# Modulation steps placed behind evictions, seven pairs of products ahead of the loop, and the order of transfers at the seam, in a two-block transformer kernel

## The chip, the core and the metric

One core of a Trainium2 chip runs the whole program. The metric is the device time of one execution in microseconds, lower being better. The engines are TensorE (PE, with its weight loads PEld), VectorE (DVE), ScalarE (ACT), GpSimd (POOL) and SyncE (SP, which here only issues transfers). Each has its own queue of instructions and works through it in order.

## What is computed

Two transformer blocks in float32 on 1024 tokens of width 1024. The first has three attentions, gates and an MLP; the second has an mLSTM, a pooling mixer and an MLP, and a modulation from a vector c. What matters here are the two MLPs and the modulation:

```python
    h = rmsnorm(x, g_mlp[l])
    hid = jnp.square(jax.nn.relu(jnp.einsum("bsd,df->bsf", h, w_mlp_in[l])))
    x = x + jnp.einsum("bsf,fd->bsd", hid, w_mlp_out[l])
...
    mod = c_act @ w_ada[l] + b_ada[l]          # c_act = silu(c), w_ada 1024 x 6144
    sh1, sc1, gt1, sh2, sc2, gt2 = jnp.split(mod, 6, axis=-1)
    h = _modulate(_rmsnorm(x, g_mix[l]), sh1, sc1)
```

The modulation depends on c alone and is wanted only by the second block, so the kernel works it out during the first block's MLP.

## The kernel before

A float32 product is made of three float32r products: each operand is split into a high part (a cast on ACT) and a low part (a subtraction on DVE or POOL), and hi·hi, hi·lo and lo·hi are added up in PSUM. The function `mlp` (from line 1211) holds both products of an MLP and is called twice, by block 1 with the modulation as its `tick` and by block 2 without one.

Both products are cut in 2 x 2 and done with Strassen and Winograd's seven products. In the first, each of 16 rounds m takes two blocks of 128 columns of w1 (`e1` and `e2`), and the seven products are of 12 matmuls each (128x128 by 128x512). P1 and P2 (`first_two`, line 1263) need only `e1` and the first half of the tokens, whose split is B11 and B21. The other five need sums of weights (`sums`, on POOL) and T1 to T4 and B22, which come from the second half of the tokens: T1 and B22 lie in `HT[1]`, T2 to T4 in six tiles of the tag `q`. `make_t` (line 1102) makes T1 as soon as the second half's norm is spread; its inner `rest` makes B22 and T2 to T4 and holds four of the six PSUM banks of the tag `mm` meanwhile.

So before the loop the kernel does P1 and P2 for m = 0 to 3, between them the norm's steps (`begin[0]`, `begin[1]`: column sums, then the spread of the result) and `rest`. In the loop, P1 and P2 for round m + 1 are done in round m from m = 3 on. A round with them has 84 matmuls, one without has 60. Evictions of a round are lines 1310, 1311, 1317, 1327, 1328, 1335, 1339 and 1340 (DVE), with 1274 for P2; line 1227 and 1228 are the two parts of a weight split. Each round saves seven results of 256 KB to DRAM through ACT's queue; four of them are put off until the next round (`later`).

The modulation is a generator, `ada` (line 1182). Each `next` loads one 128x512 block of w_ada through SP's queue and adds it, scaled, to a sum on DVE; after eight of them the next one turns the sum with four transposes, reduces it (line 1208) and adds the bias (line 1209). That makes 12 groups of nine steps. The MLP asks for two steps after the u2 and q12 evictions and two after q22, and for three (`tick2`) ahead of most products of the second stage. The order of each engine's queue is set by a scheduler that goes by the order in the program and by what it takes to be ready; it may take an instruction up earlier than it is written.

The second product (`for ch in range(4)`, four quarters of seven products) reads the saved results back as operands (`second`, two raw buffers of 1 MB, split at lines 1370 on ACT and 1371 on DVE and POOL in turn) and w2 in quarters (`quarter`, into the six tiles of T2 to T4). `upd` (line 1374) and `gather` add a product to x or to U and V7. x itself was saved to DRAM before the first product and comes back in 16 transfers at line 1356, ahead of the first quarter.

Of the kernel before, what the change touches and what calls it, by code (L numbers as in the profile page):

```python
# [14 lines left out]
AF = mybir.ActivationFunctionType  # L15
# [45 lines left out]
def block_kernel(ctx, tc, x, mem, positions, g_mix, w_in, b_gate, sinks, g_mem, w_mem_kv, w_proj_swa, w_proj_dsa,  # L61
# [1028 lines left out]
    def mlp_dram(pool):  # L1090
        d = {n: pool([P, NM, 512], tag=f"ml_{n}") for n in OUTS}
        d["x"] = pool([P, DC, S], tag="ml_x")
        return d
# [10 lines left out]
    def make_t(pool, dst, src, rs, gain, shift=None):  # L1104
# [22 lines left out]
        def rest():  # L1127
# [17 lines left out]
        rest_t.append(rest)  # L1145

# [6 lines left out]
    def x_cols(hf, e):  # L1153
# [8 lines left out]
        A.copy(xT[hf][:, e, :], pt)  # L1162

# [14 lines left out]

    mod = cst([P, 48], tag="mod")
    bada = cst([P, 48], tag="bada")  # L1180

    def ada(modp):
        badr = modp([48, P], tag="badr")
        nc.scalar.dma_start(badr, b_ada_2[0].rearrange("(k p) -> k p", p=P))
        pt = tp_bank()
        T.transpose(pt[:, :48], badr, ident[:48, :48])
        V.tensor_copy(bada, pt[:, :48])
        r0, _ = ROWS["c_2"]
        s_ = modp([P, 64], tag="silu")[:, :DC]
        A.activation(s_, cols[:, r0:r0 + 8], AF.Tanh, scale=0.5)  # L1190
        V.scalar_tensor_tensor(s_, s_, 1.0, cols[:, r0:r0 + 8], op0=OP.add, op1=OP.mult)
        V.tensor_scalar(s_, s_, 0.5, None, op0=OP.mult)
        for g in range(12):
            acc = modp([P, 512], tag="ada", bufs=1)
            for k in range(DC):
                w = modp([P, 512], tag="adaw", bufs=2)
                nc.sync.dma_start(w, w_ada_2[0, k * P:(k + 1) * P, halves(g)])
                if k == 0:
                    V.tensor_scalar(acc, w, s_[:, 0:1], None, op0=OP.mult)
                else:  # L1200
                    V.scalar_tensor_tensor(acc, w, s_[:, k:k + 1], acc, op0=OP.mult, op1=OP.add)
                yield
            yield
            m4 = mod[:, g * 4:(g + 1) * 4]
            pt = tp_bank()
            for j in range(4):
                T.transpose(pt[:, j * P:(j + 1) * P], acc[:, j * P:(j + 1) * P], ident)
            V.tensor_reduce(m4, pt.rearrange("p (j q) -> p j q", j=4), axis=AX.X, op=OP.add)
            V.tensor_tensor(m4, m4, bada[:, g * 4:(g + 1) * 4], op=OP.add)

    def mlp(PB, xt, d, w1, w2, scale, post, begin, middle, tick=lambda: None, gains=None, each=lambda i, e: None,
# [45 lines left out]
        def save(n, m, t_):  # L1257
            nc.scalar.dma_start(d[n][:, m, :], t_)

        def save_later():  # L1260
            while later:
                save(*later.pop(0))

        def first_two(m, e1, mid=None, eng=None):
# [5 lines left out]
            if mid:  # L1270
                mid()
# [3 lines left out]
            relu2(q11)  # L1275

# [12 lines left out]
        first_two(0, w_of(wp, 0, "wr", 2))  # L1289
        begin[0]()  # L1290
        first_two(1, w_of(wp, 2, "wr", 2), begin[1])
        first_two(2, w_of(wp, 4, "wr", 2), eng=G)
        rest_t.pop()()
        begin[2]()
        first_two(3, w_of(wp, 6, "wr", 2), eng=G)
        e1s[0] = w_of(wep, 0, "we", 2)
        sums(0)
        for m in range(NM):
# [12 lines left out]
            V.tensor_tensor(q12, p5, u2, op=OP.add)  # L1311
# [786 lines left out]
```

## Time and profile before

| | |
|---|---|
| time, median of 3 runs | 2725.16 us (2717.71 to 2726.5) |
| the profiled execution | 2721.95 us, span 2720.2 us |
| busy: PE, PEld, DVE, ACT, POOL | 93%, 77%, 69%, 44%, 36% of the span |
| mean granted clock of TensorE | 0.972 |
| moved by DMA | 338.6 MB, 124 GB/s over the span |

The first MLP runs from about 880 to 1600 us of the span, the second from about 2038 to the end at 2720. Busy time is that of one profiled execution, and its span is 1.75 us shorter than the time of the same execution. Matmuls are pipelined, so PE's busy share says when it had work and not how near it is to its peak; counts of matmuls say more. A row that names a releaser tells what ended the idle time before an instruction.

### The profile page before, as it was taken

The numbers are of one execution on the slowest core, as the hardware profiler recorded it, in microseconds if no ns is written. First come the engines' busy times: TensorE is split into PE (matmuls) and PEld (weight loads), VectorE is DVE, ScalarE is ACT, GpSimd is POOL, SyncE is SP. The second block draws the span as 40 slices with busy tenths as digits, with TensorE's granted clock in tenths as the row PEclk, the third lists the DMA queues.
The fourth block names the chain that finished last, engine by engine and source line by source line (L and its number), as shares of the span: only waits on it lengthen the run. The fifth ranks groups of instructions, "written<-read, shape, count | busy, mean of one in ns | idle before, by whom it ended". The sixth has DMA issues, their size and how long they took to land. (4 is left out here: it accounts for less than half of the span.)

```text
span 2720.2 us, 34915 instructions
## 1 busy us (share of the span) xinstructions
PE 2528.9 (93%) x12560; PEld 2107.4 (77%) x12560; DVE 1882.7 (69%) x3206; ACT 1197.9 (44%) x2218; POOL 988.1 (36%) x717
## 2 busy tenths in 40 slices
PE   7999999899999678888899979999997999989997
PEld 6899987788878566667688856888786788768886
DVE  7685878834455866676778896755658565578898
ACT  6575765335334433334433333323335554543433
POOL 3011123421002533333755661211334443476554
PEclk9999999999999889999999989999998999999999
DMA  3121022321155266666644301422343444753431
GB/s 114 53 61 40 25 79 90 89 61 41 63 183 179 78 203 200 202 204 230 220 170 155 109 24 51 156 63 70 120 152 97 160 150 159 250 204 134 170 109 62
DMA packets 275712, 338.57 MB, mean 124 GB/s; under 512 B 14268, under 2 KB 185044, under 8 KB 268372
## 3 DMA queue, kind: packets, MB, share of 16 engines
q1 hardware_dynamic: 234820, 253.65, 29.2%
q10 hardware_dynamic: 40720, 82.70, 8.3%
q8 instruction: 99, 1.62, 0.2%
q14 instruction: 73, 0.60, 0.1%
HBM read 250.25 MB, written 86.05 MB: 124 GB/s over the span
## 5 line engine op out<-in xcount | busy, mean ns | idle before, releaser
L1233 PE MATMUL mm<-h_hi,wh 128*128 128x512 f32 (+1 forms) x1136 | 455.5, 401 | 33.3 <-ACT wh L1227 17.2
L1235 PE MATMUL mm<-h_hi,wl 128*128 128x512 f32 (+1 forms) x1136 | 452.1, 398 | 10.5 <-DVE wl L1228 10.5
L1234 PE MATMUL mm<-h_lo,wh 128*128 128x512 f32 (+1 forms) x816 | 322.2, 395 | 0.0
L1233 PEld LDWEIGHTS mm<-h_hi,wh 128*128 128x128 f32 x1136 | 221.4, 195 | 82.2 <-ACT wh L1227 20.6
L1235 PEld LDWEIGHTS mm<-h_hi,wl 128*128 128x128 f32 x1136 | 220.7, 194 | 63.4 <-DVE wl L1228 18.2
L1227 ACT CAST wh<-q 128x1024 fp32r<-128x1024 f32 x116 | 121.7, 1052 | 331.7 <-PE mm L1234 297.7
L1234 PE MATMUL mm<-h_hi,wh 128*128 128x512 f32 (+1 forms) x624 | 244.8, 392 | 13.2 <-POOL h_hi L1371 13.2
L1228 DVE TENSOR_TENSOR wl<-q,wh 128x1024 fp32r<-128x1024 f32 x116 | 162.9, 1405 | 32.9 <-ACT wh L1227 31.3
L1234 PEld LDWEIGHTS mm<-h_lo,wh 128*128 128x128 f32 x816 | 158.3, 194 | 31.6
L1371 POOL TENSOR_TENSOR h_hi<-h_lo,h_hi 128x512 fp32r<-128x512 f32 x76 | 128.6, 1712 | 113.1 <-ACT h_hi L1370 107.9
L133 ACT CAST wh<-wr 128x1024 fp32r<-128x1024 f32 (+5 forms) x107 | 97.2, 911 | 149.7 <-PE mm L418 43.5
L1233 PE MATMUL mm<-q,wh 128*128 128x512 f32 x384 | 151.3, 394 | 10.4 <-DVE q L1119 10.4
L1235 PE MATMUL mm<-q,wl 128*128 128x512 f32 x384 | 150.2, 392 | 8.0 <-DVE wl L1228 8.0
L1234 PE MATMUL mm<-q,wh 128*128 128x512 f32 x384 | 150.9, 393 | 0.0
L1234 PEld LDWEIGHTS mm<-h_hi,wh 128*128 128x128 f32 x624 | 120.5, 193 | 37.9 <-POOL h_hi L1371 14.4
L1284 POOL TENSOR_TENSOR sa<-wr 128x512 f32<-128x512 f32 x32 | 41.7, 1303 | 264.8 <-DMA wr<-in_w_ff_dram 60.5
L134 POOL TENSOR_TENSOR wl<-wr,wh 128x1024 fp32r<-128x1024 f32 (+5 forms) x40 | 78.1, 1958 | 160.7 <-ACT wh L133 159.2
L1615 PE MATMUL mm<-h_hi,wh 128*128 128x512 f32 x320 | 132.0, 412 | 0.8 <-DVE kn L1648 0.8
L1617 PE MATMUL mm<-h_hi,wl 128*128 128x512 f32 x320 | 126.7, 396 | 0.0
L1371 DVE TENSOR_TENSOR h_hi<-h_lo,h_hi 128x512 fp32r<-128x512 f32 x76 | 120.4, 1605 | 8.3 <-ACT h_hi L1370 8.3
L1616 PE MATMUL mm<-h_lo,wh 128*128 128x512 f32 x320 | 125.5, 392 | 0.0
L1233 PE MATMUL mm<-h_lo,wh 128*128 128x512 f32 (+1 forms) x304 | 115.4, 380 | 0.6 <-ACT wh L1227 0.6
(589 smaller groups left out, 7006.9 us busy)
## 6 DMA issues: line engine op xcount, KB each, us to landing
h_lo<-ml_t SPq DMA_DIRECT2D x32, 1024.0 KB
adaw<-in_w_ada_dram SPq DMA_DIRECT2D x96, 256.0 KB
h_lo<-ml_q SPq DMA_DIRECT2D x24, 1024.0 KB
wr<-in_w_in_dram SPq DMA_DIRECT2D x42, 512.0 KB
wr<-in_w_out_dram SPq DMA_DIRECT2D x32, 512.0 KB
ml_t<-h_lo ACTq DMA_DIRECT2D x64, 256.0 KB
q<-in_w_mlp_out_dram SPq DMA_DIRECT2D x16, 1024.0 KB
ml_t<-x ACTq DMA_DIRECT2D x64, 256.0 KB
```

The source lines that it names most:

```text
L133: A.copy(hi, r)
L134: (eng or V).tensor_tensor(lo, r, raw(hi), op=OP.subtract)
L1227: A.copy(hi, r)
L1228: (eng or V).tensor_tensor(lo, r, raw(hi), op=OP.subtract)
L1233: mm(a, wt[0][:, k], b[0][:, k, sl], start=(k == 0), stop=False)
L1234: mm(a, wt[0][:, k], b[1][:, k, sl], start=False, stop=False)
L1235: mm(a, wt[1][:, k], b[0][:, k, sl], start=False, stop=(k == 3))
L1284: G.tensor_tensor(sa[:, 0:4], e2[:, 0:4], e2[:, 4:8], op=OP.add)
L1371: (G if c % 2 else V).tensor_tensor(lo[:, c], r[:, c], raw(hi[:, c]), op=OP.subtract)
L1615: mm(a, hi[:, k, :], r_hi, start=(k == 0), stop=False)
L1616: mm(a, hi[:, k, :], r_lo, start=False, stop=False)
L1617: mm(a, lo[:, k, :], r_hi, start=False, stop=(k == DC - 1))
```

## The change

- The modulation generator is set up earlier, and its preparation (the bias, the silu of c) is done in the steps of the projection ahead of MLP 1. It keeps two loads ahead: step i issues the load of step i + 2.
- Each step is asked for singly behind one eviction, and `tc.issue_after` ties its DVE instructions to come behind that eviction in DVE's queue. There are four per round of the first product: behind q12's two additions, q22's and u3's. In the second product they stand behind evictions in `upd`, `gather` and U's additions: 18 in the first quarter, 20 in each of the next two; what is left of the 108 steps after the loop's 64 ends in the third.
- P1 and P2 are done ahead for m = 4, 5, 6 and then 0 to 3. The results of 4 to 6 go to DRAM (`away`) and come back in rounds 3 to 5, which do no pair; from m = 6 on the loop does it as before.
- In `rest`, the subtractions for B22's and T3's low parts go from DVE to POOL (eight per MLP).
- In the last round, the six saves behind the first one are issued from POOL's queue instead of ACT's.
- x comes back in four transfers of 1 MB instead of 16 of 256 KB: its first half behind the first weights, q12 and t1, its second behind t2. In the first quarter the update of x's second half by U is therefore made later, from U.

```diff
-        def split_to(hi, lo, r):
+        def split_to(hi, lo, r, eng=V):
             A.copy(hi, r)
-            V.tensor_tensor(lo, r, raw(hi), op=OP.subtract)
+            eng.tensor_tensor(lo, r, raw(hi), op=OP.subtract)
...
             for c in range(4):
-                split_to(hi1[:, 4 + c, :], lo1[:, 4 + c, :], src(4 + c))
+                split_to(hi1[:, 4 + c, :], lo1[:, 4 + c, :], src(4 + c), G)
             for c in range(4):
-                split_to(t3[0][:, c, :], t3[1][:, c, :], src(c))
+                split_to(t3[0][:, c, :], t3[1][:, c, :], src(c), G)
...
+        def load(i):
+            if i < 12 * DC:
+                w = modp([P, 512], tag="adaw", bufs=2)
+                nc.sync.dma_start(w, w_ada_2[0, (i % DC) * P:(i % DC + 1) * P, halves(i // DC)])
+                ld.append(w)
...
+                w = ld.pop(0)
...
+                load(g * DC + k + 2)
+                yield
...
+    def tick1(after):
+        with tc.issue_after(after.ins):
+            next(ada_, None)
...
         def save(n, m, t_):
-            nc.scalar.dma_start(d[n][:, m, :], t_)
+            (nc.gpsimd if later and m == NM - 1 else nc.scalar).dma_start(d[n][:, m, :], t_)
...
+            if away:
+                nc.scalar.dma_start(d["away"][:, m - 4, 0, :], s1)
+                nc.scalar.dma_start(d["away"][:, m - 4, 1, :], q11)
...
-        first_two(0, w_of(wp, 0, "wr", 2))
+        first_of(4, away=True)
         begin[0]()
-        first_two(1, w_of(wp, 2, "wr", 2), begin[1])
-        first_two(2, w_of(wp, 4, "wr", 2), eng=G)
+        first_of(5, away=True)
+        begin[1]()
+        first_of(6, eng=G, away=True)
+        first_of(0)
         rest_t.pop()()
         begin[2]()
-        first_two(3, w_of(wp, 6, "wr", 2), eng=G)
+        first_of(1)
+        first_of(2)
+        first_of(3)
...
-                if m >= 3:
+                if m >= 6:
                     first_two(m + 1, e1s[m + 1])
+                elif m >= 3:
+                    for i, t_ in enumerate((s1s, q11s)):
+                        nc.sync.dma_start(t_[(m + 1) % 4], d["away"][:, m - 3, i, :])
...
-            V.tensor_tensor(q12, p5, u2, op=OP.add)
-            for _ in range(2):
-                tick()
+            tick(V.tensor_tensor(q12, p5, u2, op=OP.add))
...
-            V.tensor_tensor(q12, a, q12, op=OP.add)
+            tick(V.tensor_tensor(q12, a, q12, op=OP.add))
...
-            V.tensor_tensor(q22, p5, u3, op=OP.add)
+            tick(V.tensor_tensor(q22, p5, u3, op=OP.add))
...
-            for _ in range(2):
-                tick()
...
-            V.tensor_tensor(u3, a, u3, op=OP.add)
+            tick(V.tensor_tensor(u3, a, u3, op=OP.add))
...
-        for hf, es in ((1, range(4)), (0, range(8)), (1, range(4, 8))):
-            for e in es:
-                nc.sync.dma_start(xt[hf][:, e, :], d["x"][:, e, halves(hf)])
+        def x_back(hf):
+            for e0 in (0, 4):
+                nc.sync.dma_start(xt[hf][:, e0:e0 + 4, :], d["x"][:, e0:e0 + 4, halves(hf)])
...
+            if not late_ and e % 4 != 1 and (hf or e < 4):
+                tick(r)
             return t_
...
             b = second("q12", ch)
+            if not ch:
+                bt = second("t1", ch)
+                x_back(0)
             for e, wt in blocks(a11):
                 a = mm_bank()
                 product(a, wt, b)
                 gather(U[e], a, ch)
-                upd(1, e, a)
+                if ch:
+                    upd(1, e, a)
...
             b = second("t2", ch)
+            if not ch:
+                x_back(1)
             for e, wt in blocks(a11):
                 a = mm_bank()
                 product(a, wt, b)
-                V.tensor_tensor(U[e], a, U[e], op=OP.add)
+                if not ch:
+                    upd(1, e, U[e])
+                r = V.tensor_tensor(U[e], a, U[e], op=OP.add)
+                if e != 1:
+                    tick(r)
```

## Rows read from the trace of the kernel before

**Rows 1.** the page's slices of the span, 68 us each, TensorE in tenths.
```profile
PE   7999999899999678888899979999997999989997
```

**Rows 2.** busy us and count by engine and stage; PEclk, DMA share, GB/s.
```profile
884.00:986.00 102.00, 66.22 (x265) 52.09 (x264) 79.36 (x102) 39.12 (x63) 48.22 (x33) 0.82 0.38 122
986.00:1258.00 272.00, 240.05 (x995) 188.42 (x994) 194.00 (x252) 105.86 (x158) 97.84 (x69) 0.96 0.60 197
1258.00:1326.00 68.00, 52.96 (x212) 41.80 (x211) 37.58 (x44) 31.26 (x50) 36.85 (x20) 0.90 0.79 271
1326.00:1564.00 238.00, 238.00 (x1051) 197.07 (x1051) 201.94 (x200) 94.89 (x138) 146.31 (x72) 1.00 0.42 151
2040.00:2142.00 102.00, 82.78 (x343) 65.59 (x342) 73.65 (x93) 52.37 (x84) 48.52 (x34) 0.90 0.38 122
2142.00:2346.00 204.00, 204.00 (x902) 168.92 (x901) 113.50 (x139) 105.82 (x153) 92.33 (x66) 1.00 0.48 157
2346.00:2414.00 68.00, 56.44 (x229) 44.61 (x228) 43.89 (x48) 31.98 (x50) 43.59 (x22) 0.92 0.79 284
```

**Rows 3.** what TensorE waited for, 884 to 986: us in total, times, longest.
```profile
PE tp L1207 <- DVE ada L1201: 13.8, 2, 12.2
PE tp L1035 <- POOL st_r L127: 10.2, 1, 10.2
PE mm L1233 <- DVE q L1119: 5.7, 1, 5.7
```

**Rows 4.** DVE in order of time: start, us, what ran, idle before.
```profile
884.00 1.25 DVE L1191 SCALAR_TENSOR_TENSOR silu<-silu,cols 128x8 f32<-128x8 f32 x1
...
889.62 0.68 DVE L1274 TENSOR_TENSOR h_hi<-mm,h_hi 128x512 f32<-128x512 f32 x1
890.22 0.68 DVE L1025 TENSOR_REDUCE st_b<-tp 128x4 f32<-128x512 f32 x1
...
923.29 2.48 DVE L1119 TENSOR_TENSOR q<-h_lo,q 128x512 fp32r<-128x512 f32 x4
...
930.48 1.21 DVE L1228 TENSOR_TENSOR wl<-sa,wh 128x1024 fp32r<-128x1024 f32 x1
```

**Rows 5.** POOL in order of time, the same columns.
```profile
883.49 5.66 POOL L1114 TENSOR_TENSOR t<-h_hi,h_lo 128x512 f32<-128x512 f32 x4
```

**Rows 6.** what TensorE waited for, 2040 to 2142.
```profile
PE mm L1233 <- ACT x L1269: 8.2, 1, 8.2
PE mm L1233 <- DVE q L1119: 4.7, 1, 4.7
```

**Rows 7.** line 1310: count, ns min/median/max, first and last start.
```profile
L1310 DVE TENSOR_TENSOR h_hi<-mm,h_hi x3: 678/683/692, 939.2 to 980.3; 128x512 f32<-128x512 f32 x3
L1310 DVE TENSOR_TENSOR h_hi<-mm,h_hi x10: 681/684/687, 1005.1 to 1229.9; 128x512 f32<-128x512 f32 x10
L1310 DVE TENSOR_TENSOR x<-mm,x x3: 680/682/692, 2087.3 to 2120.2; 128x512 f32<-128x512 f32 x3
L1310 DVE TENSOR_TENSOR x<-mm,x x12: 685/692/693, 2138.3 to 2347.2; 128x512 f32<-128x512 f32 x12
```

**Rows 8.** DVE, 1060 to 1232: busy us, mean ns, idle before, releaser.
```profile
L1201 DVE SCALAR_TENSOR_TENSOR ada<-adaw,silu,ada 128x512 f32<-128x512 f32 x48 | 39.0, 812 | 39.5 <-DMA adaw<-in_w_ada_dram 39.0
L1209 DVE TENSOR_TENSOR mod<-mod,bada 128x4 f32<-128x4 f32 x7 | 8.7, 1249 | 0.0
```

**Rows 9.** what TensorE waited for, 1258 to 1326.
```profile
PE mm L1234 <- POOL h_hi L1371: 7.4, 1, 7.4
PE mm L1233 <- ACT wh L1227: 6.0, 1, 6.0
```

**Rows 10.** splits of operands on DVE and POOL, second product of MLP 1.
```profile
L1371 DVE TENSOR_TENSOR h_hi<-h_lo,h_hi 128x512 fp32r<-128x512 f32 x32 | 53.4, 1689 | 3.0 <-ACT h_hi L1370 3.0
L1371 POOL TENSOR_TENSOR h_hi<-h_lo,h_hi 128x512 fp32r<-128x512 f32 x32 | 55.9, 1767 | 43.4 <-ACT h_hi L1370 43.3
```

**Rows 11.** what SP's queue waited for, 1318 to 1564.
```profile
SPq L1364 <- DVE h_hi L1371: 137.4, 16, 13.2
```

More of the change, by code (lines that the diff above doesn't have):

```diff
@@ L1145, in make_t, with ada @@
         rest_t.append(rest)
+    mod = cst([P, 48], tag="mod")
+    bada = cst([P, 48], tag="bada")
+    def ada(modp):
+        badr = modp([48, P], tag="badr")
+        nc.scalar.dma_start(badr, b_ada_2[0].rearrange("(k p) -> k p", p=P))
+        yield
+        pt = tp_bank()
+        T.transpose(pt[:, :48], badr, ident[:48, :48])
+        V.tensor_copy(bada, pt[:, :48])
+        r0, _ = ROWS["c_2"]
+        s_ = modp([P, 64], tag="silu")[:, :DC]
+        A.activation(s_, cols[:, r0:r0 + 8], AF.Tanh, scale=0.5)
+        V.scalar_tensor_tensor(s_, s_, 1.0, cols[:, r0:r0 + 8], op0=OP.add, op1=OP.mult)
+        V.tensor_scalar(s_, s_, 0.5, None, op0=OP.mult)
+        yield
+        ld = []
+        def load(i):
[3 more added lines that the diff above has]
+                ld.append(w)
+        load(0)
+        load(1)
+        for g in range(12):
+            acc = modp([P, 512], tag="ada", bufs=1)
+            for k in range(DC):
+                w = ld.pop(0)
+                if k == 0:
+                    V.tensor_scalar(acc, w, s_[:, 0:1], None, op0=OP.mult)
+                else:
+                    V.scalar_tensor_tensor(acc, w, s_[:, k:k + 1], acc, op0=OP.mult, op1=OP.add)
+                load(g * DC + k + 2)
+                yield
+            yield
+            m4 = mod[:, g * 4:(g + 1) * 4]
+            pt = tp_bank()
+            for j in range(4):
+                T.transpose(pt[:, j * P:(j + 1) * P], acc[:, j * P:(j + 1) * P], ident)
+            V.tensor_reduce(m4, pt.rearrange("p (j q) -> p j q", j=4), axis=AX.X, op=OP.add)
+            V.tensor_tensor(m4, m4, bada[:, g * 4:(g + 1) * 4], op=OP.add)
+    modp = Pool("modp", side="right")
+    ada_ = ada(modp)
+    def tick1(after):
+        with tc.issue_after(after.ins):
+            next(ada_, None)
     xT = [hB([P, DC, 512], tag=n) for n in ("h_hi", "h_lo")]
@@ L1162, in x_cols @@
         A.copy(xT[hf][:, e, :], pt)
+        if e == 2:
+            next(ada_)
     mlp_d = mlp_dram(drm)
@@ L1176, in block_kernel, with mlp @@
     HT[1] = h_tiles(hBp)
[L1179 to L1211, printed above, removed]
+    def mlp(PB, xt, d, w1, w2, scale, post, begin, middle, tick=lambda ins: None, gains=None, each=lambda i, e: None,
             parts=((0, 0, 512), (1, 0, 512))):
@@ L1376, in upd @@
             if scale is None:
-                V.tensor_tensor(t_, a, t_, op=OP.add)
+                r = V.tensor_tensor(t_, a, t_, op=OP.add)
             else:
-                V.scalar_tensor_tensor(t_, a, scale[:, e:e + 1], t_, op0=OP.mult, op1=OP.add)
-            return t_
-        def tick2():
-            for _ in range(3):
-                tick()
+                r = V.scalar_tensor_tensor(t_, a, scale[:, e:e + 1], t_, op0=OP.mult, op1=OP.add)
+            if not late_ and e % 4 != 1 and (hf or e < 4):
+                tick(r)
+            return t_
         def gather(to, a, ch):
             if ch:
-                V.tensor_tensor(to, a, to, op=OP.add)
+                r = V.tensor_tensor(to, a, to, op=OP.add)
+                if to is V7[0] or to is V7[2]:
+                    tick(r)
             else:
@@ L1437, in mlp @@
                 gather(U[e], a, ch)
-                upd(1, e, a)
+                if ch:
+                    upd(1, e, a)
             a12 = quarter(ch, 1, 0)
-            tick2()
-            b = second("t1", ch)
+            b = second("t1", ch) if ch else bt
             for e, wt in blocks(s_):
@@ L1534, in post_mlp1 @@
         if hf == 0:
-            for _ in ada_["it"]:
+            for _ in ada_:
                 pass
@@ L1561, in h2_half @@
         yield
-    ada_ = {}
     def begin1():
         stp.close()
-        ada_["it"] = ada(pools["mod"])
     def middle1():
         pools["stm"] = Pool("stm", side="right", n512=2)
-    def tick1():
-        next(ada_["it"], None)
-    pools["mod"] = Pool("modp")
     mlp(hBp, xT, mlp_d, w_mlp_in[0], w_mlp_out[0], None, post_mlp1,
         (lambda: next(pend), lambda: next(pend), begin1), middle1, tick1, gsq)
-    pools["mod"].close()
     drm.close()
@@ L1691, in block_kernel @@
     pools["stm"].close()
+    modp.close()
     pt = tp_bank()
```

17 lines of the change are left out of this document (7 added, 10 removed).

## Prediction

> **What bounds the kernel now.** I read the page's slices first: TensorE is busy nine tenths or more in 27 of 40, and nine of the other thirteen lie in the two MLPs: a run of seven from 884 us on, which is the first MLP's beginning and loop, and single ones at the second's [rows 1]. So the question is not how fast the matmuls are but where they are missing. For that I took the busy time by stage, with matmuls counted [rows 2]. The stretch 1326 to 1564 is full: 1051 matmuls in 238 us, 0.2264 us each; 2142 to 2346 gives the same (902 in 204). With that price every other stretch has a loss, its length less its matmuls times 0.2264:
>
> - MLP 1, beginning (884 to 986): 102 − 60.0 = 42.0 us
> - MLP 1, loop over m (986 to 1258): 272 − 225.3 = 46.7
> - MLP 1, seam between the two products (1258 to 1326): 68 − 48.0 = 20.0
> - MLP 2, beginning (2040 to 2142): 102 − 77.7 = 24.3; its loop: 0; its seam (2346 to 2414): 68 − 51.8 = 16.2
>
> That is 149 us in all, the most that this change can touch. The losses include the clock: the granted clock averages 0.82 in the first of these stretches against 1.00 in the full ones [rows 2], so part of it ran at 1.2 instead of 2.4 GHz, behind TensorE's waits of up to 12 us [rows 3].
>
> Then what ended the waits. At the beginning of MLP 1 they are the modulation's transposes waiting for its sum, the norm's power on POOL, and the splits of the rest of T2 to T4 [rows 3]. In MLP 2, which has no modulation, only a PSUM eviction on ACT and the T4 split stand out [rows 6]. The loop is best read by its period, the distance between two u2 evictions (line 1310) [rows 7]: 84 matmuls need 19.0 us at the full rate, 60 need 13.6. MLP 1 takes (1229.9 − 1005.1)/9 = 25.0 us for 84, MLP 2 (2347.2 − 2138.3)/11 = 19.0. For 60 (m = 0, 1) MLP 1 takes 20.6, MLP 2 16.5. The difference between the MLPs is the modulation: 48 accumulations of 0.81 us within 172 us, some 7 an iteration, with 39.0 us of DVE waiting for their loads [rows 8]. The code asks for 4 steps an iteration, so they run ahead of their place: the first come between the last evictions of the projection [rows 4].
>
> **The change, part by part.** The numbers are what I expect to be left of each loss.
>
> Beginning, per MLP. The short loop rounds m = 0, 1 take 2 × (20.6 − 13.6) = 14 us of the 42.0 in MLP 1 and 2 × (16.5 − 13.6) = 5.8 of the 24.3 in MLP 2, so the beginnings proper lose 28 and 18.5. Three more pairs of P1 and P2 (m = 4 to 6) put 3 × 24 × 0.2264 = 16.3 us of matmuls beside the norm and the rest of T; they are not added work, since the loop does three pairs fewer. Eight subtractions go from DVE to POOL: 0.62 us each on DVE, 1.42 on POOL by its nearest additions [rows 4, 5], so DVE's chain is 5 us shorter and POOL has 11 us more, behind which the T4 sums queue. In MLP 1 the modulation's preparation leaves the norm's path: the reduce started at 890.2 after DVE had done the silu and two steps from 884.0 on [rows 4], about 4 us. Against it: the rest holds 4 of 6 PSUM banks, so pairs 1 to 3 have two, and their evictions queue behind the rest on ACT and DVE, the wait of 8.2 us in [rows 6]. I keep 8 us in each MLP; bounds 2 (all covered) and 20 (MLP 2 as it is).
>
> The Trainium skill (GPSIMD Engine Reference, 8. Key points) speaks against the POOL splits: POOL shares its SBUF interfaces with DVE and contends with DVE instructions that have two SBUF inputs. The trace agrees: such a split takes DVE 0.62 us with POOL mostly idle and 1.69 us in the second product, where POOL does the same at 1.77 [rows 4, 10]. By that rule eight DVE instructions beside the moved ones lose 1.07 each, 8.6 us, which would turn the 5 us gained into 3.6 lost; it lies within my bounds of 2 to 20.
>
> The rounds m = 0 to 5 now all have 60 matmuls, five periods. MLP 2 pays 16.5 − 13.6 = 2.9 each: 5 × 2.5 = 12 (bounds 4 and 20). In MLP 1 each has four modulation steps and 12.4 us of DVE work for 13.6: MLP 2's 113.5/204 × 19.0 = 10.6 us [rows 2], less the pair's eviction and split (0.68 + 1.21 [rows 4]), plus 3.7 for four steps (a group of nine is 8 × 0.81 + 1.25 + a reduce of 0.68 = 8.4 us [rows 4, 8]). I take 5 × 4 = 20; bounds 5 × 1.5 and 5 × 7, the last what m = 0, 1 lose now. Two reloads of 256 KB per round come with them, 4.25 MB in 16 to 18 us, about 250 GB/s; the seams reach 271 to 284 [rows 2], so no bound by itself.
>
> Long rounds of MLP 1: nine. Four pinned steps make 10.6 + 3.7 = 14.3 us of DVE in 19.0, and each load is issued two steps early. 0.6 us each is left, 5 us; bounds 0 and 27, 3 us each, half of what it is.
>
> Seams. The 16 reads of x come as four and behind the first weights, q12 and t1, so the wait for the first weights (6.0 in MLP 1) shrinks; the split of t1, which waited on POOL for 7.4, is traced before the first blocks [rows 9]. Left: 5 each, between 1 and 15. The last six saves go to POOL's queue ahead of its sums for the second block. No row has a DMA issued by POOL: between 0 and a 1.42 us addition each, 8.5 us; I take 2, within the 5, since the sums wait for their weights anyway. The Trainium skill (DMA: Bandwidth & Descriptors, Latency and other measured facts) gives 1 us instead of 0.6 to the first byte on that queue; six times 0.4 would make it 2.4 us, which no row here shows.
>
> New cost, the second product of MLP 1. Of 108 steps the loop takes 64; 44 and the end go between its evictions. Five groups of 8.4 us are 42 us of DVE. DVE now works 201.9 of 238 us there [rows 2], 64.2 in the 75.7 us of a quarter, with 11 free; the quarters get 18, 20 and 7 steps: 17, 19 and 7 us. Above the free time that is 6 + 8 + 0 = 14, less about 2 that the first quarter's copies on ACT leave: 12. Bounds: 0, and 42 if nothing is free.
>
> Sum: MLP 1 keeps 8 + 20 + 5 + 5 + 12 = 50 of 108.7, MLP 2 8 + 12 + 5 = 25 of 40.5. The gain is 58.7 + 15.5 = 74 us. The profiled execution took 2721.95 us (span 2720.2), 3 below the median; 2721.95 − 74 = 2648.
>
> **Rivals.**
>
> - All covered: beginnings 2, rounds 1.5 and 0.8 each, long rounds 0, seams 2, steps in the second product 0. Left 11.5 + 8 = 19.5 of 149.2: gain 130, 2592. For it: MLP 2's full loop. Against it: POOL and ACT chains that no part shortens.
> - DVE binds in the second product and the short rounds: 42 us there, since the steps have two SBUF inputs like the 1.69 us splits [rows 10], and 35 us in the rounds. MLP 1 keeps 8 + 35 + 5 + 5 + 42 = 95, MLP 2 25: gain 29, 2693. For it: DVE is at 85% there.
> - The pairs ahead do not do what they are for: the banks hold them up and both beginnings lose 20. 2648 + 24 = 2672. For it: the PSUM wait of [rows 6]; against it: pairs 4 to 6 and 0 come before the banks are taken.
> - Slower: SP's queue. In the second product SP stands up to 13.2 us at the next operand load, waiting for DVE's split [rows 11]. A modulation load behind it comes late, its step holds DVE in order, and behind the step queue evictions and the very splits SP waits for. With DVE's free time used up (12 left over above), each us of wait per step costs 45. From (74 + 8)/45 = 1.8 us per step on the kernel is slower; the loop's waits are 39.5 us over some 55 steps, 0.7 each [rows 8]. At 2.3 us it is 2648 + 104 = 2752. Against it: two steps of lead, 5 us and more.
>
> **How the numbers follow.** Forecast 2648, own range 2620 to 2680: 0.52. All covered 0.12, DVE bound 0.18, banks 0.11, slower by SP 0.07. 2600 to 2702 leaves out the slower case, a quarter of the DVE case and half of the covered one, under 0.2. 0.3% (8 us) is what a measurement can tell: faster 0.89 (all but SP and the worst of the DVE case), within it 0.04, slower 0.07.
>
> **What would show it.** Right: periods of line 1310 near 19.5 (nine) and 16 to 18 (five) in MLP 1; no wait of TensorE for the modulation's sum; the x reads behind q12 and t1; DVE at 95% or more in the first two quarters of the second product, with TensorE short gaps. Wrong: rounds of 60 still at 20; waits of 6 us and more at the beginnings; DVE waiting for modulation loads in the second product.

## The result and the profile after

| | us, median | runs | ratio to before, 95% interval |
|---|---|---|---|
| kernel before | 2725.3 (2717.7 to 2726.5) | 4 | |
| changed kernel | 2683.2 (2682.1 to 2684.8) | 4 | 0.9852 (0.9833 to 0.9870) |

The change makes the kernel 42 us faster; 74 were forecast. The profiled execution has a span of 2680.7 us (2720.2 before) and a mean granted clock of 0.977 (0.972).

TensorE's slices on the page of the changed kernel (the span in 40 slices of 67 us; tenths of busy time), to be held against [rows 1]:

```profile
PE   7999999999999889997999969999998899999997
```

Where [rows 1] had a run of seven slices under nine tenths, MLP 1 has three now: two eights at its beginning and a seven at its seam (1206 to 1273). The six at 1541 is where [rows 1] has its seven at 1564, behind the stretches listed here, and the two eights at 2011 are the beginning of MLP 2. By stage, with the columns of [rows 2] (busy time by engine, instructions in brackets, then granted clock, DMA share, GB/s); beginnings, rounds and seams are parted at evictions of u2, line 1344:

```profile
884.00:939.60 55.60, 42.95 (x170) 33.88 (x169) 35.28 (x51) 29.20 (x51) 27.46 (x21) 0.88 0.27 82
939.60:1029.50 89.90, 78.13 (x325) 63.85 (x325) 61.33 (x77) 33.73 (x50) 44.25 (x29) 0.91 0.66 215
1029.50:1223.90 194.40, 188.32 (x822) 154.63 (x821) 151.66 (x178) 95.31 (x140) 84.43 (x58) 0.98 0.63 205
1223.90:1292.00 68.10, 50.90 (x195) 40.02 (x194) 52.40 (x56) 25.74 (x40) 40.52 (x26) 0.86 0.76 281
1292.00:1360.00 68.00, 68.00 (x301) 56.20 (x301) 62.38 (x62) 27.18 (x40) 43.90 (x22) 0.99 0.59 203
1360.00:1462.00 102.00, 95.81 (x419) 78.19 (x418) 98.39 (x111) 34.66 (x49) 52.91 (x26) 0.98 0.60 206
2000.00:2057.00 57.00, 44.88 (x194) 36.14 (x193) 39.68 (x54) 35.78 (x60) 29.37 (x22) 0.91 0.34 105
2057.00:2141.80 84.80, 76.93 (x315) 60.54 (x314) 41.48 (x55) 34.53 (x51) 39.31 (x31) 0.96 0.55 180
2141.80:2325.70 183.90, 182.33 (x803) 150.37 (x802) 107.26 (x131) 96.31 (x140) 81.92 (x59) 1.00 0.51 170
2325.70:2380.00 54.30, 47.05 (x187) 37.54 (x186) 48.18 (x36) 23.47 (x36) 37.92 (x24) 0.91 0.75 275
```

Length less matmuls times 0.2264 us gives the loss of each stage, as in the prediction. The kernel before is parted anew for this, at its own evictions of u2 (line 1310); the second column has its stretches and their matmuls. Short rounds are two before and five after. The stretch of long rounds has twelve before and nine after, and with them the last round, which is short. The second product's stage ends at 1462 after the change; the next 68 us lose nothing (301 matmuls).

| stage | before: stretch, matmuls | before | forecast | after |
|---|---|---|---|---|
| MLP 1 beginning | 884 to 939.2, 129 | 26.0 | 8 | 17.1 |
| MLP 1 short rounds | to 980.3, 112 | 15.7 (two) | 20 (five) | 16.3 |
| MLP 1 long rounds | to 1279.8, 1116 | 46.8 | 5 | 8.3 |
| MLP 1 seam | to 1326, 115 | 20.2 | 5 | 24.0 |
| MLP 1 second product | to 1564, 1051 | 0 | 12 | 7.1 |
| MLP 2 beginning | 2040 to 2087.3, 126 | 18.8 | 8 | 13.1 |
| MLP 2 short rounds | to 2120.2, 124 | 4.8 (two) | 12 (five) | 13.5 |
| MLP 2 long rounds | to 2360.8, 1061 | 0.4 | 0 | 2.1 |
| MLP 2 seam | to 2414, 163 | 16.3 | 5 | 12.0 |
| sum | | 149.0 | 75 | 113.5 |

All of the gain lies in MLP 1. The losses of MLP 2, which has no modulation, add up to 40.3 us before and 40.7 after, where 25 were forecast: what the other parts of the change win there at the beginning and the seam they lose in the rounds. The table accounts for 35.5 of the 39.5 us between the two spans; 2.9 of the rest is that the first matmul of MLP 1 runs at 877.07 instead of 879.99.

The rounds and the second product came out near their terms. The seams miss by 26.0 us, the beginnings by 14.2. What ended TensorE's waits there (first MLP 1's beginning, then its seam, MLP 2's beginning, MLP 2's seam; total, times, longest):

```profile
PE mm L1255 <- DVE q L1120: 7.2, 1, 7.2
PE mm L1257 <- DVE wl L1250: 5.4, 1, 5.4
...
PE mm L1257 <- DVE wl L1250: 9.7, 1, 9.7
PE mm L1255 <- ACT wh L1249: 3.8, 1, 3.8
PE tp L1189 <- DVE ada L1182: 3.6, 1, 3.6
...
PE mm L1255 <- DVE q L1120: 11.0, 1, 11.0
PE mm L1257 <- DVE wl L1250: 1.1, 1, 1.1
...
PE mm L1257 <- DVE wl L1250: 7.3, 3, 4.9
```

Against [rows 9] the split of t1 on POOL (7.4 us) is gone and the first weights wait 3.8 instead of 6.0; in their place stands a split of weights on VectorE, and the modulation's transposes now wait in the seam too. The runs below follow these waits. Stages whose code is the same differ by up to 3 us from kernel to kernel, and the second product of MLP 1 by more (it loses 6 to 12 us in the kernels that have the modulation's steps there). Differences in us are differences of the ratios to before, times 2725; each ratio has an interval of about 0.0018 (5 us) either way, so a difference between two kernels under some 7 us is not shown by the times alone.

### The profile page after: what moved, and what is told of

It is laid out like the page before. It is cut to its first block, busy times and chain, and to the rows that moved or that the text cites. A ratio compares the mean times of both kernels' runs of the same rounds, so it can differ in the third digit from the quotient of the medians.

```text
span 2680.7 us, 34925 instructions
## 1 busy us (share of the span) xinstructions
PE 2519.1 (94%) x12560; PEld 2105.3 (79%) x12560; DVE 1891.5 (71%) x3192; ACT 1198.4 (45%) x2218; POOL 1001.1 (37%) x743
## 5 line engine op out<-in xcount | busy, mean ns | idle before, releaser
L1250 DVE TENSOR_TENSOR wl<-q,wh 128x1024 fp32r<-128x1024 f32 x116 | 191.7, 1655 | 25.0 <-ACT wh L1249 23.6
L1256 PEld LDWEIGHTS mm<-h_hi,wh 128*128 128x128 f32 x624 | 121.9, 195 | 24.2
L1250 DVE TENSOR_TENSOR wl<-we,wh 128x1024 fp32r<-128x1024 f32 x50 | 81.0, 1620 | 57.2 <-ACT wh L1249 53.1
L1257 PE MATMUL mm<-h_lo,wl 128*128 128x512 f32 (+1 forms) x304 | 115.6, 380 | 0.2 <-DVE wl L1250 0.2
```

What stands on the lines that cost most here:

```text
L1250: (eng or V).tensor_tensor(lo, r, raw(hi), op=OP.subtract)
L1256: mm(a, wt[0][:, k], b[1][:, k, sl], start=False, stop=False)
L1257: mm(a, wt[1][:, k], b[0][:, k, sl], start=False, stop=(k == 3))
```

## Experiments: the seams

Line 1250 splits 128x1024 weights. Nine such splits lie in MLP 1's seam, seven in MLP 2's (ns min, median, max):

```profile
L1250 DVE TENSOR_TENSOR wl<-q,wh x9: 1209/1212/10416, 1235.3 to 1290.2; 128x1024 fp32r<-128x1024 f32 x9
L1250 DVE TENSOR_TENSOR wl<-q,wh x7: 1207/1803/13519, 2334.1 to 2377.1; 128x1024 fp32r<-128x1024 f32 x7
```

One in each takes about ten times its normal 1.21 us. The timeline of POOL beside it, MLP 1 (start, us), with VectorE's line last:

```profile
1242.75 1.10 POOL L1280 DMA_DIRECT2D ml_t<-h_lo  x2
1243.87 4.75 POOL L1462 TENSOR_TENSOR q<-q,q 128x1024 f32<-128x1024 f32 x2
1248.56 4.68 POOL L1483 TENSOR_TENSOR q<-q,q 128x1024 f32<-128x1024 f32 x2
1253.21 4.63 POOL L1484 TENSOR_TENSOR q<-q,q 128x1024 f32<-128x1024 f32 x2
1257.81 1.25 POOL L1401 TENSOR_TENSOR h_lo<-h_lo,h_lo 128x512 fp32r<-128x512 f32 x1
...
1249.73 12.69 DVE L1250 TENSOR_TENSOR wl<-q,wh 128x1024 fp32r<-128x1024 f32 x3 [8.61 <-ACT wh L1249]
```

The first of the three splits begins at 1249.73 and takes 10.42, to 1260.15, when TensorE's wait for it ends (1250.48 + 9.72). That is 1.1 us after the end of POOL's train (1259.06), about its own length, so it seems to have got nothing done beside the train. POOL's instructions lie end to end at some 2.35 each; the last of the six saves that the change moved to POOL is issued right ahead of them.

**seam_dve**

```diff
-                if e == 0:
+                if e == (0 if ch else 2):
+                    with tc.issue_after(lastwl[0].ins):
...
-                        G.tensor_tensor(a21[:, q_], a11[:, q_], a21[:, q_], op=OP.subtract)
-                        G.tensor_tensor(a11[:, q_], s_[:, q_], a11[:, q_], op=OP.subtract)
+                            (G if ch else V).tensor_tensor(a21[:, q_], a11[:, q_], a21[:, q_], op=OP.subtract)
+                            (G if ch else V).tensor_tensor(a11[:, q_], s_[:, q_], a11[:, q_], op=OP.subtract)
```

> Edit: in the first quarter the four subtractions that update a21 and a11 (lines 1483 and 1484, 9.3 us without a gap on POOL) run on VectorE, behind the split of the second block of the sum. My theory: that train of POOL instructions is what holds VectorE's split for 10.4 us (MLP 1) and 13.5 us (MLP 2), so no split takes over 3.5 us there, TensorE's waits for it fall from 9.7 and 4.9 to under 3 and 2, and the time falls by 7 to 12, to about 2674. Rival: the waits come from POOL's sum being late behind POOL's six saves; then TensorE still waits 6 us or more in MLP 1's seam, for the sum, and the time is within 3 us of 2683.

lastwl is the split of the block that was traced last; the tie to it stands in all four quarters, the change of engine in the first alone. Measured 2671.8 us, ratio 0.9816 (0.9798 to 0.9833), 10 us under the changed kernel. TensorE's waits for the split in MLP 1's seam, and the splits themselves there and in MLP 2's:

```profile
PE mm L1259 <- DVE wl L1250: 5.1, 4, 1.8
```

```profile
L1250 DVE TENSOR_TENSOR wl<-q,wh x11: 1203/1221/3416, 1234.9 to 1298.6; 128x1024 fp32r<-128x1024 f32 x11
L1250 DVE TENSOR_TENSOR wl<-q,wh x11: 1205/1809/4170, 2326.4 to 2379.8; 128x1024 fp32r<-128x1024 f32 x11
```

No split is over 4.2 us (0.7 more than expected), and the longest wait for one is 1.8 us in MLP 1 and 2.1 in MLP 2; in total the waits fall from 9.7 to 5.1 and from 7.3 to 4.8, less than expected. The seams lose 15.1 and 9.0 us instead of 24.0 and 12.0. Without POOL's train the long split is gone, and so are some 10 us. Why this train and no other holds a split so long, the next run was to say.

**saves_act**

```diff
-            (nc.gpsimd if later and m == NM - 1 else nc.scalar).dma_start(d[n][:, m, :], t_)
+            nc.scalar.dma_start(d[n][:, m, :], t_)
```

> Undoes one part: the saves of the last round go back from POOL's queue to ACT's. By the theory that the back-to-back POOL instructions starve VectorE, the train still runs and one split still takes 8 us or more, only some 5 us earlier; time within 4 us of 2683, on the slower side if ACT's splits queue behind the saves. By the rival, that the late sum is the cause, all splits take under 3.5 us, TensorE's waits in the seams fall by 8 us together and the time is about 2674.

Measured 2681.8 us, ratio 0.9852 (0.9837 to 0.9868): no gain, no loss. The train still runs, but the splits beside it are short, against my theory (VectorE and POOL, MLP 1's seam):

```profile
1248.67 5.65 DVE L1250 TENSOR_TENSOR wl<-q,wh 128x1024 fp32r<-128x1024 f32 x2 [10.44 <-ACT wh L1249]
...
1241.56 2.39 POOL L1462 TENSOR_TENSOR q<-q,q 128x1024 f32<-128x1024 f32 x1 [8.55 <-DMA q<-in_w_mlp_out_dram]
...
1247.51 5.72 POOL L1483 TENSOR_TENSOR q<-q,q 128x1024 f32<-128x1024 f32 x2
1253.19 6.18 POOL L1484 TENSOR_TENSOR q<-q,q 128x1024 f32<-128x1024 f32 x2
```

The two share: POOL takes 2.86 and 3.09 each, VectorE's two splits 5.65 together. The rival is half right. Without the saves no split is starved, but the time stays: the sum starts only 2.3 us earlier (1241.6), since it waits for the weights' transfer, and TensorE's waits in this seam are 8.0 for splits, 4.5 for weights and 4.5 for transposes, 17.0 in all as in the changed kernel (17.1). The two seams by stage:

```profile
1222.90:1291.00 68.10, 51.12 (x194) 39.72 (x193) 51.31 (x57) 25.65 (x40) 40.84 (x20) 0.85 0.79 285
2323.50:2377.80 54.30, 47.28 (x188) 36.84 (x188) 42.34 (x36) 23.48 (x36) 37.20 (x18) 0.94 0.75 275
```

They lose 24.2 and 11.7 us, against 24.0 and 12.0. So a train alone does not starve a split, and ending the starving this way gained nothing: beside the same train the splits are late either way, in MLP 1 in one wait of 9.7 us or in four of at most 3.7, 8.0 together. In MLP 2 their waits do fall, from 7.3 to 4.1, but waits of 2.9 for weights come up on ACT, whose queue now has the saves. The last run asked whether POOL's own DMA issues ahead of the train do the starving.

**pool_dma_probe**: saves_act, and in the second quarter

```diff
+            if ch == 1:
+                with tc.issue_after(lastg[0].ins):
+                    pd = [nc.gpsimd.dma_start(d["away"][:, i // 2, i % 2, :P], ident) for i in range(6)]
+            with tc.issue_after(pd[-1].ins) if pd else nullcontext():
                 for c in (0, 2):
                     G.tensor_tensor(s_[:, c:c + 2], a21[:, c:c + 2], a22[:, c:c + 2], op=OP.add)
```

> saves_act (no DMA issued by POOL in the seams), and in the second quarter of both MLPs POOL issues six small DMAs (128x128 of the identity into the store of the pairs, by then unused) right ahead of its sums. In saves_act VectorE's splits beside that train of sums take 2.9 and 3.2 us, and POOL's instructions 2.9 to 3.1. Theory: a train of POOL sums right behind POOL's own DMA issues gets the memory alone, as in the changed kernel's seams (POOL 2.33 an instruction, VectorE's split 10.4 and 13.5 us): then a split in the second quarter takes 8 us or more and POOL's sums 2.3 to 2.4. Rival: the DMAs are not the cause, and the splits stay at 3.5 us or less.

The splits of line 1250 in saves_act in that stretch, then POOL and VectorE of the probe (MLP 1):

```profile
L1250 DVE TENSOR_TENSOR wl<-q,wh x2: 2923/3053/3183, 1305.8 to 1311.2; 128x1024 fp32r<-128x1024 f32 x2
```

```profile
1302.55 3.41 POOL L1466 DMA_DIRECT2D ml_a<-ident  x6
1305.97 4.76 POOL L1469 TENSOR_TENSOR q<-q,q 128x1024 f32<-128x1024 f32 x2
1310.67 4.75 POOL L1490 TENSOR_TENSOR q<-q,q 128x1024 f32<-128x1024 f32 x2
...
1309.00 8.76 DVE L1251 TENSOR_TENSOR wl<-q,wh 128x1024 fp32r<-128x1024 f32 x1 [4.22 <-ACT wh L1250]
```

A split of 8.76 us in MLP 1 and one of 9.24 in MLP 2, where saves_act has at most 3.18 in both, and POOL's instructions at 2.38 instead of 2.9 to 3.1. (This kernel was run once.) The cause of the starved split is shown in both directions: POOL's DMA issues followed at once by a train of its two-input sums. The other runs agree: in the eight kernels that have both the six saves on POOL and the train there, VectorE's longest split of weights takes 10.4 to 13.5 us; in the kernel before, in saves_act and in seam_dve it takes 2.4, 3.4 and 4.2. It is not the issues themselves: a split of the probe that runs while POOL issues, at 1303.56, takes 1.22 us. What in the hardware makes it so stays open.

**x_first**

```diff
-        def x_back(hf):
...
+        for hf, es in ((1, range(4)), (0, range(8)), (1, range(4, 8))):
+            for e in es:
+                nc.sync.dma_start(xt[hf][:, e, :], d["x"][:, e, halves(hf)])
...
-            if not ch:
-                bt = second("t1", ch)
-                x_back(0)
...
-                if ch:
-                    upd(1, e, a)
+                upd(1, e, a)
```

> Undoes one part: the 16 reads of x go back ahead of the first weights of the second product, and t1's operand and the evictions into x to their places of before. By the prediction's terms the first weights are late again (6.0 us in MLP 1) and t1's split is late: 5 more in each seam, 2693. Rival: the seam's losses (24 us now, 20.2 before in MLP 1) are set by POOL's train of sums, and the reads are hidden behind it: 2683 within 3.

Measured 2690.4 us, ratio 0.9895 (0.9878 to 0.9911), 12 us above the changed kernel. TensorE's waits in MLP 1's seam:

```profile
PE mm L1255 <- ACT wh L1249: 10.0, 2, 8.0
PE mm L1257 <- DVE wl L1250: 9.7, 1, 9.7
```

The first weights are 8.0 us late instead of 3.8, and the 9.7 for the split comes on top. So the reordering was worth about its 10 us, as the prediction said. By stage it shows in MLP 2, whose seam loses 20.3 us here and 12.0 in the changed kernel; in MLP 1 it is 24.9 and 24.0, where the later weights and the wait of 3.6 us for the modulation's sum, which is missing here, nearly cancel.

## Experiments: the modulation's steps

TensorE waits for the last step of a group, ahead of its transposes, seven times (view of the tile ada on TensorE, changed kernel):

```profile
  DVE ada L1182: 25.0, 7
```

The kernel before has 26.4 us in nine such waits, so the change has hardly touched them. The queueing holds VectorE's steps behind evictions, but nothing holds the transposes: on TensorE they stand right behind a product, and the last step waits for an eviction there.

**tp_pinned** (lastmm is the last matmul that a product traced)

```diff
+            with tc.issue_after(lastmm[0].ins):
                 for j in range(4):
                     T.transpose(pt[:, j * P:(j + 1) * P], acc[:, j * P:(j + 1) * P], ident)
```

> Against the changed kernel, 2683.2 us, with TensorE's 25.0 us in 7 waits ahead of the modulation's transposes (line 1189). Edit: the four transposes of a group are queued on TensorE behind the last matmul traced, so a whole product (12 matmuls, 2.7 us) further back than the eviction behind which the last step runs. My theory: the waits come from the transposes' place in TensorE's queue alone, so they fall below 5 us and the time by about 20, to 2663 (2658 to 2672). Rival: the wait only shows that VectorE is behind there; then TensorE waits at the same places for an eviction or a split on VectorE instead, and the time stays within 4 us of 2683.

Measured 2676.1 us, ratio 0.9828 (0.9810 to 0.9847), 6.5 us under the changed kernel. The waits fell to 13.4 us in five. In the rounds two of the three, of 8.1 and 3.7 us, are gone (one of 3.3 stays), and the losses there (short and long) fall from 24.6 to 16.4. In the seam and the second product, where the transposes did not move in TensorE's queue (523, 683 and 831 matmuls behind the last u2 eviction, against 524, 684 and 832), four waits stay (3.6, 1.6, 1.4, 3.5). Place was half of the cause.

**sum_early**: tp_pinned, and

```diff
                 load(g * DC + k + 2)
-                yield
+                if k != DC - 2:
+                    yield
             yield
+            yield
```

> Edit: as tp_pinned, and the last two steps of a group stand behind one eviction, so the sum is finished one eviction earlier while the transposes keep their place. My theory: the waits that tp_pinned left (3.3 us at 1010, 3.6, 1.6, 1.4 and 3.5 us in the seam and the second product) come from a sum that VectorE, 98% busy there, reaches late by less than one product, so all but some 2 us of these 13.4 go: 8 to 12 us below tp_pinned (2676), about 2666. Rival: VectorE is behind for good in the second product, and the waits turn into waits for evictions and splits there: 2674 or more.

Measured 2673.8 us, ratio 0.9826 (0.9809 to 0.9843), no different from tp_pinned. The waits for the sum halve again (6.6 us in 4), but from the first eviction of u2 to the last the rounds take 280.8 us instead of 276.5: TensorE's waits for splits there rise from 10.1 to 13.2, so two steps behind one eviction seem to delay the splits. By the time the rival holds: less waiting for the sum brought nothing.

**unpinned**

```diff
-        with tc.issue_after(after.ins):
-            next(ada_, None)
+        next(ada_, None)
```

> Undoes one part: the modulation's steps keep their places in the program (four a round, the loads two steps ahead), but are no longer queued on VectorE behind the evictions. My theory: the queueing is what the long rounds gained by; without it the steps run ahead of their place again, the nine long periods of MLP 1 go from 19.9 back towards 25 and the five short ones from 18 towards 20.6, and the second product is free of steps: 2683 + 9 x 4.6 + 5 x 2.5 - 7 - 10 (the waits for transposes there) = 2720 (2705 to 2735). Rival: the loads two steps ahead do most of it, and the rounds stay under 21: 2690 or less.

Measured 2714.5 us, ratio 0.9979 (0.9969 to 0.9989), 35 us above the changed kernel, of the 40 that the whole change is worth by the ratio. All the other parts together thus bring 6 us (3 to 8). The evictions of u2 from the first long period on (first and last start), unpinned and changed kernel:

```profile
L1343 DVE TENSOR_TENSOR h_hi<-mm,h_hi x10: 683/684/692, 1051.8 to 1263.5; 128x512 f32<-128x512 f32 x10
```

```profile
L1344 DVE TENSOR_TENSOR h_hi<-mm,h_hi x11: 681/692/692, 1029.5 to 1223.9; 128x512 f32<-128x512 f32 x11
```

211.7/9 = 23.5 us a long period, against 20.0 (the eleventh eviction, 14.5 later, ends the last round, which has 60 matmuls). The loads two steps ahead, which this kernel keeps, do not bring it. It also shows what the steps cost behind the loop, since here none is left by then. Its seam in MLP 1, then its second product:

```profile
1277.10:1345.20 68.10, 57.99 (x242) 46.52 (x242) 57.79 (x50) 29.82 (x47) 43.75 (x27) 0.92 0.79 292
1345.20:1583.20 238.00, 238.00 (x1052) 197.07 (x1051) 209.22 (x198) 90.25 (x131) 158.18 (x78) 1.00 0.36 128
```

The losses are 13.3 and 0 us, against 24.0 and 7.1: the steps cost some 18 us there, 11 of them within the seam's stretch, where the first quarter begins. The saves on POOL, the train and the reordered reads are as in the changed kernel.

## Experiments: the beginnings

**t4_first** (sums holds the last of the four sums on POOL)

```diff
-            for c in range(4):
-                split_to(hi1[:, 4 + c, :], lo1[:, 4 + c, :], src(4 + c), G)
-            for c in range(4):
-                split_to(t3[0][:, c, :], t3[1][:, c, :], src(c), G)
+            for c in range(4):
+                first(4 + c, t1[c])
+            with tc.issue_after(sums[0].ins):
+                for c in range(4):
+                    split_to(hi1[:, 4 + c, :], lo1[:, 4 + c, :], src(4 + c), G)
+                for c in range(4):
+                    split_to(t3[0][:, c, :], t3[1][:, c, :], src(c), G)
```

> Edit: POOL's eight moved splits (B22 and T3, 1.24 us each) are queued behind its four sums for T4, not among them. My theory: T4's VectorE work waits 5.3 and 3.5 us for the last sum, which is queued behind POOL's splits, and the four PSUM banks stay taken meanwhile; so TensorE's waits for the T4 split, 7.2 us in MLP 1 and 11.0 in MLP 2, fall by 3 to 6 us each and the time by 6 to 10, to about 2675. Rival: the splits that are now last are those of T3 and B22, needed first, so the wait only changes its name; the time is then within 3 us of 2683.

In the changed kernel T4's last sum stands behind four T3 splits and one of B22 on POOL, and VectorE waits for it with the T4 chain:

```profile
911.89 2.48 DVE L1120 TENSOR_TENSOR q<-mm,q 128x512 fp32r<-128x512 f32 x4
912.27 4.97 POOL L1120 TENSOR_TENSOR q<-h_lo,q 128x512 fp32r<-128x512 f32 x4
...
918.41 1.27 POOL L1115 TENSOR_TENSOR t<-h_hi,h_lo 128x512 f32<-128x512 f32 x1
...
919.71 0.70 DVE L1144 TENSOR_TENSOR mm<-t,mm 128x512 f32<-128x512 f32 x1 [5.34 <-POOL t L1115]
```

Measured 2676.9 us, ratio 0.9838 (0.9820 to 0.9855), 4 us under the changed kernel. TensorE's waits (MLP 1, then MLP 2):

```profile
PE mm L1259 <- ACT h_hi L1296: 6.5, 1, 6.5
PE mm L1261 <- DVE wl L1254: 2.0, 1, 2.0
...
PE mm L1259 <- ACT x L1296: 6.8, 1, 6.8
```

The waits of 12.6 and 12.1 become 8.5 and 8.0, 4.1 less each, and what is late next is the eviction on ACT: line 1296 copies P1 of the next pair, and in MLP 2 it runs at 2033.4, behind all but four of the rest's casts and copies on ACT. That is the wait of 8.2 us in [rows 6], still there.

**splits_dve**

```diff
-                split_to(hi1[:, 4 + c, :], lo1[:, 4 + c, :], src(4 + c), G)
+                split_to(hi1[:, 4 + c, :], lo1[:, 4 + c, :], src(4 + c))
...
-                split_to(t3[0][:, c, :], t3[1][:, c, :], src(c), G)
+                split_to(t3[0][:, c, :], t3[1][:, c, :], src(c))
```

> Undoes one part: the eight splits of B22 and T3 at each beginning go back from POOL to VectorE. By the prediction's terms VectorE's chain is 5 us longer in each MLP: 2693 at the most. By the rule that POOL and VectorE contend, or because T4's last sum no longer queues behind the splits (5.3 and 3.5 us of wait), it is 2 to 4 us shorter in each: 2677. I expect the two to cancel: 2683 (2678 to 2688), TensorE's two waits in MLP 1's beginning at 10 to 14 us together, now 12.6.

Measured 2684.2 us, ratio 0.9869 (0.9854 to 0.9884): 5 us above the changed kernel, not beyond the intervals. TensorE's waits in MLP 1's beginning (6.4 for ACT's eviction, 5.7 for the T4 split, 0.6) are 12.7 as before: VectorE's longer chain stands where POOL's queue stood.

**four_pairs**

```diff
-        first_of(4, away=True)
-        begin[0]()
-        first_of(5, away=True)
-        begin[1]()
-        first_of(6, eng=G, away=True)
-        first_of(0)
-        rest_t.pop()()
-        begin[2]()
-        first_of(1)
-        first_of(2)
-        first_of(3)
+        first_of(0)
+        begin[0]()
+        first_of(1)
+        begin[1]()
+        first_of(2, eng=G)
+        rest_t.pop()()
+        begin[2]()
+        first_of(3, eng=G)
...
-                if m >= 6:
+                if m >= 3:
                     first_two(m + 1, e1s[m + 1])
-                elif m >= 3:
...
```

> Undoes one part: four pairs of P1 and P2 ahead instead of seven, none stored away; rounds m = 0 to 2 have 60 matmuls in the loop, the others 84. By the prediction's terms the three pairs bring 10 us in each beginning and cost 3 short periods of 2.5 to 4: net 3 in MLP 1 and 2.5 in MLP 2, so undone 2689. My theory after the stages of the changed kernel (MLP 2: beginning and short rounds lose 23.6 before and 26.6 after): a round of 60 takes 17 us on the other engines against 19 for one of 84, so a pair taken out of a round frees 2 us and not 5.4, and the pairs are worth nothing: 2680 (2673 to 2687), with MLP 2's beginning and short rounds together at 22 to 26. Rival: they cover the beginning fully as meant, and undone costs 10 an MLP: 2703.

Measured 2674.6 us, ratio 0.9833 (0.9815 to 0.9851), 5 us under the changed kernel. Beginning and rounds of MLP 1, then of MLP 2, by stage:

```profile
884.00:930.00 46.00, 29.68 (x108) 22.23 (x107) 30.77 (x46) 22.04 (x40) 29.47 (x22) 0.81 0.13 36
930.00:1218.60 288.60, 276.48 (x1214) 227.97 (x1213) 226.07 (x259) 137.57 (x202) 125.21 (x87) 0.98 0.62 200
...
1987.40:2044.40 57.00, 41.23 (x167) 31.92 (x166) 38.22 (x50) 31.45 (x53) 38.62 (x29) 0.85 0.28 84
2044.40:2317.50 273.10, 269.07 (x1184) 221.61 (x1183) 156.35 (x192) 139.18 (x202) 122.72 (x89) 1.00 0.49 163
```

Losses 21.5 and 13.8, 19.2 and 5.0, against 17.1 and 24.6, 13.1 and 15.6 of the changed kernel. The three further pairs save 4.4 and 6.1 us at the beginnings and cost 10.8 and 10.6 in the rounds. A pair holds 5.4 us of matmuls, but in MLP 2 a round without it takes 17.0 us (84.8/5) against 19.0 with it, since the short rounds wait for splits on ACT and VectorE (5.7 and 2.1 us in the five): the pair frees 2 us there, and at the beginning, where TensorE has waits of up to 11 us anyway, 16.3 us of matmuls cover 4 to 6.

## Experiments: the causes together

**best_seven** holds the edits of sum_early, seam_dve and t4_first; **best_four** those and four_pairs.

> The edits of sum_early, seam_dve and t4_first together, with the seven pairs of the changed kernel. If the causes are separate, the gains add up: 2683 - 16 (transposes) - 10 (seams) - 4 (T4) = 2653 (2648 to 2660). If one wait hides behind another, less: 2663 or more.

> best_seven with four pairs ahead, as in four_pairs. If the three further pairs are worth less than they cost (four_pairs gained 5 against the changed kernel), it is some 5 us under best_seven: 2648. Rival: with T4's sums first and the transposes out of the way the beginning is short of matmuls again, and the seven pairs win by 3 or more.

Measured 2659.3 us, ratio 0.9771 (0.9755 to 0.9787), and 2650.3 us, ratio 0.9733 (0.9719 to 0.9748). The gains of the three edits over the changed kernel (7.1, 9.8, 3.8) sum to 20.7; together they bring 22, so the causes are separate as far as the times can tell. With four pairs it is 10 more, and here the intervals don't touch. best_four is 73 us under the kernel before, 32 under the changed one. Its seams (230 matmuls in 68.0 us, 204 in 54.3) keep 15.9 and 8.1 us of 24.0 and 12.0, with the transfers busy 0.87 and 0.86 of the time; the beginnings keep 17 and 16.

## Why the prediction was right and wrong

Sign and range were right: faster, and 2683 lies within 2600 to 2702. The gain was little more than half of the forecast (42 of 74), and 2683 lies 3 above the forecast's own range. The range held because it was wide: the modulation's queueing brought its part, and the 15.5 us forecast for MLP 2 did not come at all. The table of the result says which steps failed.

- **The seams** (10 forecast, 36.0 measured) are the term that failed. I priced them by the two waits of [rows 9] and by the saves' time in POOL's queue (2 us, at most 8.5). These prices held: a save takes 0.54 to 0.75 us and the six delay the sum by 2.3, the first weights are 2.2 us less late and t1's split no longer waits. Two things were put at nothing. One is VectorE's weight splits beside POOL's train of sums: seam_dve, which takes the train away, brings the seams to 15.1 and 9.0. The other is the modulation's steps of the first quarter, which I counted in the second product alone: in unpinned, which has none there, MLP 1's seam loses 13.3, close to MLP 2's 12.0. That the six saves starve one split I had not foreseen either (waits of 9.7 and 4.9 us at a time); with the saves back on ACT the seams lose as much, so it is not shown that the starving costs time. The clock falls in these stretches too (0.86 and 0.91).
- **No wait of TensorE for the modulation's sum** was named as a sign of being right; there are 25.0 us of it in seven waits, about as many as before (26.4). I had followed every queue that the steps are moved past on VectorE and SP, but not the transposes on TensorE, which belong to the same step. tp_pinned takes half of the waits away by their place alone.
- **The beginnings** (16 forecast, 30.2 measured): a sign of being wrong came true, waits of 6 us and more (7.2 and 11.0). The mechanism was the rival "banks hold the pairs", in part. I had noted that the T4 sums queue behind POOL's splits and gave it no price; it is 5.3 and 3.5 us of VectorE's wait, and t4_first takes 4.1 us off TensorE's waits in each. The other half is ACT's queue, which the term "evictions queue behind the rest" names and under-sizes: 6.5 and 6.8 us, near the 8.2 of [rows 6], which was the row to take.
- **More pairs ahead**: the sum had both sides, 10.5 us won at MLP 2's beginning (18.5 to 8) against 6 lost in its short rounds. The cost came out (13.5/5 = 2.7 us a round in MLP 2, where I had read 2.9 and taken 2.5 without a reason; 16.3/5 = 3.3 in MLP 1). The gain was mis-sized: four_pairs shows 4.4 and 6.1 us won at the beginnings by 16.3 us of matmuls, against 10.8 and 10.6 lost in the rounds.
- **The rounds of MLP 1** were right, and with them most of the gain: long periods of 20.0 us (19.5 forecast), short ones of 18.0 (16 to 18), from 25.0 and 20.6 in [rows 7]. unpinned shows that the queueing brings 35 us.
- **The second product** was right in kind and somewhat low: 12 us were forecast for the steps behind the loop, and 7.1 there and some 11 in the seam's stretch were measured. VectorE is busy 98.39 of 102 us from 1360 to 1462 and 92% of the 68 us before, with short waits of TensorE. The rival that VectorE binds (42 us there) is refuted. So is SP's queue: VectorE waits 3.3 us in three waits for the modulation's loads in the whole kernel, against the 39.0 us in the loop of [rows 8], and 0.8 us once from 1292 on.

The Trainium skill (GPSIMD Engine Reference, 8. Key points) was weighed against the eight moved splits, where I worked out 8.6 us lost. That was a wrong reading: the Trainium skill names VectorE instructions with two SBUF inputs there, and the splits that VectorE does beside the moved ones read one operand from PSUM. They take 0.62 us each at 911.89, beside POOL's four from 912.27 on, so the trace agrees with it, and taking the eight back in splits_dve gained nothing. The rule that does bear on the seams is in the Trainium skill (SBUF — State Buffer, Who interferes with whom): a VectorE instruction with two SBUF inputs and a GpSimd instruction that reads SBUF lock each other out for a whole instruction, and the one that issues first wins. The ordinary trains agree (2.9 and 3.2 us for a split of 1.21 beside a POOL sum of 2.4: one instruction waited for). The starved splits go beyond it: 10.4 us is four of POOL's sums in a row.

## What to carry to other kernels

When work is moved within a queue, list for each instruction of the step who reads its result, and see to that reader's place too: the transposes waited for the sum as long after this change as before it. Take work out of a loop only where the round gets shorter by it, since a round that other engines hold at 17 us gives back 2 of the 5.4 that were taken out. Keep VectorE's splits on the path clear of a train of POOL's two-input sums: that was worth 10 us here, and moving POOL's DMA issues to ACT was worth nothing. Where a change has many parts, look for a place that has some of them without the others, as MLP 2 here.

## What the runs showed of the hardware that I had not expected

A VectorE split of 128x1024 that takes 1.21 us alone, and 2.9 to 3.4 beside an ordinary train of POOL sums, takes 8.8 to 13.5 when POOL has issued DMAs right ahead of the train; POOL's sums then run at some 2.35 us each instead of 2.9 to 3.1. A split during the issues themselves takes its normal time (1.22 us). A DMA issue costs POOL 0.54 to 0.75 us.
